# Small products at other places in TensorE's order: a later joined block in the second half, row transposes inside xa, two gate banks moved

## The chip, the cores and the metric

The kernel runs on one core of a Trainium2 chip. The core has five engines that run their own instruction streams: TensorE (PE in the profile; its weight loads are listed apart as PEld), VectorE (DVE), ScalarE (ACT), GpSimd (POOL) and SyncE (SP), which issues most of the DMAs. The metric is device time in microseconds (us) of one execution. A difference of less than about half a per cent between two versions can hardly be told from none.

## The reference

One layer of a decoder trunk on 1024 tokens of width 1024, in float32. Cut to what matters here:

```python
h = rms_norm(x, norm_mix)
xa, ga, q, f, v, g, m_a, m_b = split(h @ w_in)            # 8 projections, 1024 wide each
xa  = causal_depthwise_conv(xa, conv_w, conv_b)           # 4 taps
r   = sigmoid(blockdiag(xa, w_r) + b_r)                   # blocks of 256
i   = sigmoid(blockdiag(xa, w_i) + b_i)
a   = exp(-8 * r * softplus(-lam))
hr  = scan(h_t = a_t * h_(t-1) + sqrt(1 - a_t**2) * (i * xa)_t)
y_a = hr * gelu(ga)
# HGRN2, 8 heads of 128, chunks of 32 tokens, a state S of 128 x 128 per head
F   = lb + (1 - lb) * sigmoid(f);   K = (1 - lb) * sigmoid(-f);   Q = silu(q)
o_t = Q_t @ S_t  with  S_t = F_t * S_(t-1) + K_t (outer) v_t
y_b = rms_norm(o, hg_norm) * silu(g)
y   = sigmoid(m_a) * y_a + sigmoid(m_b) * y_b
x   = x + y @ w_out
x   = x + square(relu(rms_norm(x, norm_mlp) @ w_up)) @ w_down
out = rms_norm(x, norm_final)
```

## The kernel before

**Products.** A float32 product is made of three products of rounded parts: `mm3` issues H·H, L·H and H·L (lines 132, 133, 134). `split` makes the parts of a weight (`wH` a cast on ScalarE, L87, `wL` a subtraction on VectorE, L88). A "step" of a projection is six matmuls of 128x512.

**The mixer.** Tokens come in two halves (c = 0, 1) of T = 512, and heads in four pairs (p = 0..3) of 256 columns: eight blocks i = 4c + p. For each there is a generator `stage(i)`, which issues the work ahead of its recurrence: the products for `v` of block i−1 in four quarters tt (24 matmuls of 256 columns each, with the call `between(tt)` after a quarter), `xa` with its convolution, `q`, `f`, and `rg_lru` with the two gates (`pr`, `pi`, six matmuls each, for s = 0 and 1). `hgrn(i)` issues the recurrence of block i. It makes decay products on VectorE (`kk`, `kc`, `kb`, `qa`, `qb`, `qf`) and small products on TensorE: the level blocks `pt1`, `pt2`, `pt8`; the "joined block" of 32 rows (L634) and of 64 rows (L645) of the scores `sc`; transposes `pk` of `kk` (L671); `pkv` (L681), from which VectorE makes the states `sn` (L692); the output `po` (L706, L709). After it comes the norm of `po`: squares with a sum on ScalarE (L713), their power on GpSimd (`hrs`, L721), `normalised()` (L728). `on_T` later transposes the result (L384) and stores it in `od`. In stages 1 to 3 the rows of the second half are transposed as well (`transposed`, L162).

**The order.** While `hgrn(i)` runs, `stage(i+1)` is taken forward in pieces: `go(n)` issues its next n steps. The table

```python
GO = (26, 5, 2, 1, 1)
```

says how many steps go ahead of the level blocks, then of the joined block, of `pk`, of `pkv` and of `po`. In the mixer TensorE's instructions are pinned to the order in which they are written; the other engines' orders are made by a scheduler.

**Banks.** PSUM is shared in three groups: `pj` with four banks, `sc` with two, `hg` with two. A product waits until the bank that it takes in turn has been read. Projections take `pj`; `pt1`, `pt2` and the 64 rows take `sc`; `pt8`, the 32 rows, `pk`, `pkv`, `po` and all transposes take `hg`.

**GpSimd's other work.** From the fifth block on, `combos_on(n)` puts in n pieces that form sums of weights for the gate phase; a long piece has two products (L324), two more of `stT` and eight sums `r`.

**The gate phase.** The four gates' products (ga, m_a, m_b, g) are made in 16 "quads" of 512 x 512 by a Strassen-like scheme, of which `own` lists fourteen, 2 to 15. `gate_step(q, step)` issues step 0 to 6 of a quad: 12 matmuls into a bank X (`pj`), Y (`sc`) or Z (`hg`). Steps 0 to 2 end in a copy on ScalarE, steps 3 to 5 in an add on VectorE (L1000), step 6 in a copy. `gate_work(q)` then applies the gate's function to the whole quad (128x2048): for quad 2, the first of `own`, it is the gelu, with a TS (L1028), a product (L1029), tanh, two products (L1032) and one by the RG-LRU's `h`. `with_o(p)` multiplies the merged gate `g2` by `o` (L1057). The next quad's operands are loaded by `load_quad` (L906, in the order `in_turn`) and split (`wA`, `ws…`). The output projection and the MLP follow.

Of the kernel before, what the change touches and what calls it, by code (L numbers as in the profile page):

```python
# [14 lines left out]
ALU = mybir.AluOpType  # L15
# [17 lines left out]
OUT_TILES = 8  # L33
QUADS = 16
LEVELS = (2, 8)
GO = (26, 5, 2, 1, 1)
OWN_BEFORE = 2


# [5 lines left out]
def trunk(ctx: ExitStack, tc: tile.TileContext, x, wts, mlp, pv, gains, mask_f, mask_u, out):  # L45
    nc = tc.nc
    V, A, G, PE = nc.vector, nc.scalar, nc.gpsimd, nc.tensor
# [13 lines left out]
    def bank(tag, name):  # L61
        return ps.tile([P, 512], F32, tag=tag, name=name, bufs={"pj": 4, "sc": 2, "hg": 2}[tag])
# [3 lines left out]
    for i in range(NC * NPAIR):  # L66
        at = (0, 1, 2, 3, 4, 6, 5)
# [98 lines left out]
    hT = []  # L166
# [192 lines left out]
    def v_steps(c, p, got, between):  # L359
        v = mt("v", f"v_{c}{p}", (P, 4, 256))  # L360
        w = [next_w(), next_w()]
        for tt in range(4):
            pp = bank("pj", f"pv_{c}{p}_{tt}")
            for k in range(8):
                hh, hl = kt(hT[c], k)
                cut = slice(tt * P, (tt + 1) * P)
                cols = slice((k % 4) * 256, (k % 4 + 1) * 256)
                wh, wl = w[k // 4]
                mm3(pp[:, :256], hh[:, cut], hl[:, cut], wh[:, cols], wl[:, cols], k == 0, k == 7)
                if k % 2:  # L370
# [58 lines left out]
    def rg_lru(c, p, got, xc, xh, xl):  # L429
        wh, wl = next_w()  # L430
        nm = f"{c}{p}"
        w, ig, e = (mt(t, f"{t}{nm}", (P, 2, T)) for t in ("rw", "ri", "rr"))
        a = mt("h", f"a{nm}", (P, 2, T))
        last = []

        def on_act(*a, **k):
            ins = A.activation(*a, **k)
            if last:
                how = mybir.DependencyInfo(mybir.DependencyClass.NoSync, mybir.DependencyReason.DATA)
                tc.add_manual_dep(ins.ins, last[-1].ins.name, how, reason="on_act")  # L440
            last.append(ins)

        for s in range(2):
            u = 2 * p + s
            pr, pi = bank("pj", f"pr{c}{u}"), bank("pj", f"pi{c}{u}")
            for o, k0 in ((pr, 0), (pi, 2)):
                for k in range(2):
                    cols = slice((k0 + k) * 256 + s * P, (k0 + k) * 256 + (s + 1) * P)
                    mm3(o, wh[:, cols], wl[:, cols], xh[:, k, :], xl[:, k, :], k == 0, k == 1)
                yield  # L450
            on_act(w[:, s, :], pr, AF.Sigmoid, bias=pvt[:, PV_BR + u : PV_BR + u + 1])
            on_act(ig[:, s, :], pi, AF.Sigmoid, bias=pvt[:, PV_BI + u : PV_BI + u + 1])
# [49 lines left out]
    def hgrn(c, p, got, go):  # L502
        q1, f, kk = got["q1"], got["f"], got["kk"]
# [87 lines left out]
        t4 = nxt.rearrange("p (a b) -> p a b", b=4)  # L591
        q4 = qb.rearrange("p a (b c) -> p a b c", c=c1)
        level_q(q4, t4, g1, c1)
        go(GO[0] - (10 if first else OWN_BEFORE))
        pt1 = blocks(kk, lambda k: q1[:, 16 * k : 16 * k + 16, :], "1")
        if not first:
            go(OWN_BEFORE)
# [27 lines left out]
                op1=ALU.add,  # L625
            )

        go(GO[1])
# [38 lines left out]
        go(GO[2])  # L667
# [9 lines left out]
        go(GO[3])  # L677
# [6 lines left out]
        for s, u in both:  # L684
            sn = sns[:, s]
            states.append([scar[:, u, :]] + [sn[:, n, :] for n in range(4)])
            for n in range(nkv):
# [3 lines left out]
                else:  # L691
# [5 lines left out]
                        op0=ALU.mult,  # L697
                        op1=ALU.add,
                    )
        go(GO[4])  # L700
        po = [bank("hg", f"po{c}{u}") for _, u in both]
        for s, u in both:
            for n in range(4):
# [46 lines left out]
    def v_of(i):  # L750
        def between(tt):
            if tt == 0:
                gots[i - 1]["tail"]()
            if tt == 1:
                on_T(*where(i - 2), gots[i - 2])
            for n in {(2, 2): (1,), (3, 0): (2,), (3, 2): (3,)}.get((i, tt), ()):
                with tc.high_priority(400):
                    transposed(xn1[n], hT[1], n, f"x1{n}")

        yield from v_steps(*where(i - 1), gots[i - 1], between)  # L760

    def stage(i):
# [3 lines left out]
            yield from v_steps(c, p, got, lambda tt: None)  # L766
        elif i > 1:
            yield from v_of(i)
        px = yield from project_steps(c, f"xa{c}{p}")
        xc, xps = conv_in(c, p, px)  # L770
        if i == 0:
            parameters()
# [200 lines left out]
        loads.append(ins)  # L973

    GQ = 2 * QUADS
    gwork, gb, gbank, ge, live = {}, {}, {}, {}, {}
    SIGN = (1.0, -1.0, -1.0, 1.0)

    def gp_tile(tag, name):
# [2 lines left out]
    def gate_step(q, step):  # L982
# [12 lines left out]
        if step < 3:  # L995
            ge[q, step] = gp.tile([P, T], F32, tag="e", name=f"ge{step}_{q}", bufs=4)
            A.copy(ge[q, step], o)
        elif step < 6:
            at, e = {3: (0, 0), 4: (2, 1), 5: (3, 2)}[step]
            V.tensor_tensor(out=b[:, at, :], in0=o, in1=ge.pop((q, e)), op=ALU.add)  # L1000
        else:
            A.copy(b[:, 1, :], o)

# [9 lines left out]
    def gate_work(q):  # L1013
# [11 lines left out]
        elif gate == 2:  # L1025
            t = gp_tile("sg", f"sg{q}")
            A.activation(t, b, AF.Square)
            V.tensor_scalar(t, t, 0.044715, 1.0, op0=ALU.mult, op1=ALU.add)  # L1028
            V.tensor_tensor(out=t, in0=t, in1=b, op=ALU.mult)  # L1029
            A.activation(t, t, AF.Tanh, scale=GELU_C)  # L1030
            for cut, one in ((slice(0, 4, 3), 1.0), (slice(1, 3), -1.0)):
# [22 lines left out]

    def with_o(p):
        o = load_4(od[p], f"o{p}")
        V.tensor_tensor(out=live["g2"], in0=live["g2"], in1=o, op=ALU.mult)  # L1057

    yt = {}

# [39 lines left out]
    gwork[own[0]]["c"]()  # L1100
    live["g2"] = gp_tile("b", "g2_0")
    nc.sync.dma_start(live["g2"], g2d)
    with_o(0)
    for q in own:
        n = q + 1
        if n > own[1] and n < QUADS:
# [1 line left out]
        for step in (1, 2, 5, 4, 6) if q == own[0] else (0, 1, 2, 3, 4, 5, 6):  # L1108
# [3 lines left out]
            gate_step(q, step)  # L1112
            if q == own[0] and step == 4:
                gate_step(own[1], 0)
            pinned[0] = False
            if n == QUADS:
                if step == 2:
# [10 lines left out]
            for k in {2: ("sums", "a", "b"), 5: ("c",), 6: ("d",)}.get(step, ()):  # L1128
                if q > own[0]:
                    gwork[n][k]()  # L1130
                elif k != "a":
                    with tc.high_priority(300):
                        gwork[n][k]()
        gate_work(q)
    close_gp()
    close_tp()
    close_w1()
# [388 lines left out]
```

## Time and profile before

| | |
|---|---|
| time, median of 3 runs | 1584.06 us (1580.7 to 1586.53) |
| time of the profiled execution | 1579.99 us |
| its span, first to last instruction | 1578.2 us |
| mean granted TensorE clock | 0.997 |
| TensorE, matmul | 1528.8 us, 97% |
| VectorE | 1208.0 us, 77% |
| ScalarE | 819.6 us, 52% |
| GpSimd | 162.0 us, 10% |
| DMA | 280.07 MB, mean 177 GB/s |

The first of the gate phase's products in a bank X starts at 579.2 us; what lies before is the mixer. A row of the trace gives the start (us), the length, the engine, the source line, the operation with out<-in (numbers of names left out), its shape and, in square brackets, how long the engine stood idle before it and which instruction of which engine ended that. In a row that groups several instructions (x4) the length reaches from the first's start to the last's end, or is their sum. A busy TensorE may still be slow: the granted clock in the view of windows tells.

### The profile page before, as it was taken

How to read it: one execution, taken by the hardware profiler on the slowest of the kernel's cores; microseconds unless marked ns; L12 is line 12 of the kernel's file. 1: busy time of each engine (PE TensorE's matmuls, PEld its weight loads, DVE VectorE, ACT ScalarE, POOL GpSimd, SP SyncE). 2: the span in 40 equal slices, each digit the busy share in tenths (PEclk: the TensorE clock that was granted, in tenths of full speed). 3: DMA queues.
4: the chain of work that ended last, by engine and by line, in shares of the span. 5: the costliest groups of instructions: out<-in, count | busy, mean ns of one | idle time of the engine just before them, and what ended most of it. 6: DMA issues, size and time to landing. Idle time of an engine off the chain costs nothing.

```text
span 1578.2 us, 23146 instructions
## 1 busy us (share of the span) xinstructions
PE 1528.8 (97%) x9072; PEld 1275.6 (81%) x9072; DVE 1208.0 (77%) x1706; ACT 819.6 (52%) x1341; POOL 162.0 (10%) x187
## 2 busy tenths in 40 slices
PE   7989999999999999999999998999999999999998
PEld 6878888888787887888888876888888878888886
DVE  5797586696876928786866489987778888888877
ACT  5646656567475634444444277776777632211113
POOL 1011110234437600000000000000000000000000
PEclk9999999999999999999999999999999999999999
DMA  6333222232433364424237863766666575666642
GB/s 235 99 99 108 68 96 93 84 132 94 134 134 121 108 253 161 159 96 141 92 126 271 290 224 112 277 255 251 250 246 252 224 272 225 250 254 255 254 198 107
DMA packets 75341, 280.07 MB, mean 177 GB/s; under 512 B 7776, under 2 KB 20192, under 8 KB 62304
## 3 DMA queue, kind: packets, MB, share of 16 engines
q1 hardware_dynamic: 72208, 267.58, 46.6%
q10 hardware_dynamic: 3024, 11.01, 1.9%
q8 instruction: 71, 1.16, 0.3%
q14 instruction: 38, 0.31, 0.1%
HBM read 193.63 MB, written 84.93 MB: 177 GB/s over the span
## 4 chain that ended last, share of the span: by engine, by line
PE 75%; DVE 14%; ACT 7%; issue 2%; DMA 1%; POOL 0%; DVEq 0%; POOLq 0%; SPq 0%; ACTq 0%
PE dX L132 3%; PE dX L133 3%; PE dX L134 3%; PE uX L132 3%; PE uX L133 3%; PE uX L134 3%; PE gX L132 3%; PE gX L134 3%; PE gX L133 3%; PE dY L132 2%; PE dY L133 2%; PE dY L134 2%; PE uY L132 2%; PE uY L134 2%; PE uY L133 2%
## 5 line engine op out<-in xcount | busy, mean ns | idle before, releaser
L88 DVE TENSOR_TENSOR wL<-raw,wH 128x1024 fp32r<-128x1024 f32 x100 | 123.9, 1242 | 86.5 <-ACT wH L87 86.5
L87 ACT CAST wH<-raw 128x1024 fp32r<-128x1024 f32 x100 | 104.9, 1049 | 68.4 <-PE po L133 29.2
L1435 DVE TENSOR_TENSOR acc<-acc,dX 128x512 f32<-128x512 f32 x128 | 85.0, 682 | 29.5 <-PE dX L134 28.3
L87 ACT CAST wA<-q 128x512 fp32r<-128x512 f32 x46 | 28.4, 620 | 132.5 <-PE dX L134 101.4
L1435 DVE TENSOR_TENSOR acc<-acc,dY 128x512 f32<-128x512 f32 x64 | 43.4, 685 | 15.6 <-PE dY L134 14.5
L132 PE MATMUL po<-wH,y 128*128 128x512 f32 x128 | 50.1, 391 | 0.0
L133 PE MATMUL po<-wL,y 128*128 128x512 f32 x128 | 50.0, 391 | 0.0
L134 PE MATMUL po<-wH,y 128*128 128x512 f32 x128 | 50.0, 391 | 0.0
L1300 ACT ACTIVATE b<-b 128x512 f32<-128x512 f32 x48 | 30.1, 630 | 29.6 <-DVE b L1299 29.5
L155 POOL TENSOR_TENSOR rstd_h<-rstd_h,mhalf 128x1 f32<-128x1 f32 x8 | 5.6, 699 | 384.2 <-DVE rstd_h L154 384.2
L411 DVE SCALAR_TENSOR_TENSOR xc<-xp,pvt,xc 128x512 f32<-128x512 f32 x48 | 40.4, 862 | 0.0
L713 ACT ACTIVATE on<-po 128x128 f32<-128x128 f32 x64 | 16.8, 278 | 43.8 <-PE po L709 43.8
L88 DVE TENSOR_TENSOR wA<-q,wA 128x512 fp32r<-128x512 f32 x46 | 31.5, 685 | 9.3 <-ACT wA L87 9.2
L918 DVE TENSOR_TENSOR s<-q,q 128x512 f32<-128x512 f32 x46 | 31.5, 687 | 3.0 <-DMA q<-mlp_in 2.5
L324 POOL TENSOR_TENSOR stt<-r,stt 128x256 fp32r<-128x256 f32 x16 | 23.2, 1469 | 93.0 <-ACT stt L323 93.0
L923 DVE TENSOR_TENSOR s<-q 128x512 f32<-128x512 f32 x46 | 31.5, 685 | 0.3
L1301 ACT ACTIVATE b<-b 128x512 f32<-128x512 f32 x48 | 30.1, 630 | 1.1
L1000 DVE TENSOR_TENSOR gb<-gY,ge 128x512 f32<-128x512 f32 x14 | 9.7, 690 | 26.0 <-PE gY L134 25.4
L134 PEld LDWEIGHTS po<-wH,y 128*128 128x128 f32 x128 | 24.0, 188 | 5.0
L133 PEld LDWEIGHTS po<-wL,y 128*128 128x128 f32 x128 | 24.0, 188 | 4.9
L132 PEld LDWEIGHTS po<-wH,y 128*128 128x128 f32 x128 | 24.0, 188 | 4.8
L706 PE MATMUL po<-v,scT 128*128 128x128 f32 x128 | 24.6, 286 | 2.7 <-DVE sn L692 2.7
(2528 smaller groups left out, 5424.9 us busy)
## 6 DMA issues: line engine op xcount, KB each, us to landing
raw<-wts_in SPq DMA_DIRECT2D x96, 512.0 KB, 3.6
q<-mlp_in SPq DMA_DIRECT2D x92, 512.0 KB, 3.7
x<-x_in SPq DMA_DIRECT2D x8, 512.0 KB, 6.0
hd<-ri SPq DMA_DIRECT2D x16, 256.0 KB, 2.9
od<-onT ACTq DMA_DIRECT2D x8, 512.0 KB, 4.7
cdT<-stT SPq DMA_DIRECT2D x16, 256.0 KB, 3.5
o<-od SPq DMA_DIRECT2D x4, 1024.0 KB, 7.1
h<-hd SPq DMA_DIRECT2D x4, 1024.0 KB, 4.8
```

Source lines behind the costliest of these rows:

```text
L87: keep(A.copy(h, src))
L88: keep(V.tensor_tensor(out=lo, in0=src, in1=h.bitcast(F32), op=ALU.subtract))
L132: pin(PE.matmul(o, ah, bh, start=first, stop=False, **how))
L133: pin(PE.matmul(o, ah, bl, start=False, stop=False, **how))
L134: pin(PE.matmul(o, al, bh, start=False, stop=last, **how))
L411: ins = V.scalar_tensor_tensor(xc[:, s, :], xp[:, j : j + T], pvt[:, PV_CW + 8 * j + u : PV_CW + 8 * j + u + 1], xc[:, s, :], op0=ALU.mult ...
L706: pin(PE.matmul(on_ps, scT[:, 4 * s + n, :], vn(s, n), start=True, stop=only))
L918: V.tensor_tensor(out=sa[:, 0, :], in0=a21, in1=a22, op=ALU.add)
L923: V.tensor_tensor(out=sb[:, 0, :], in0=a21, in1=a11, op=ALU.add)
L1300: A.activation(b[:, at, :], b[:, at, :], AF.Relu, scale=-1.0 if at == 2 else 1.0)
L1301: A.activation(b[:, at, :], b[:, at, :], AF.Square)
L1435: V.tensor_tensor(out=dst, in0=dst, in1=banks[bk, pr], op=op)
```

## The change

Nothing is added to or taken from the work; every engine has as many instructions as before. What changes is where some stand.

```diff
-GO = (26, 5, 2, 1, 1)
+GO = (26, 5, 3, 1, 1)
+GO_FIRST = (16, 5, 2, 1, 2)
+GO_SECOND_HALF = (26, 7, 3, 1, 1)
...
-            pp = bank("pj", f"pv_{c}{p}_{tt}")
+            pp = bank("pj" if tt < 3 else "sc", f"pv_{c}{p}_{tt}")
...
-            pr, pi = bank("pj", f"pr{c}{u}"), bank("pj", f"pi{c}{u}")
+            pr, pi = (bank(("pj", "sc")[s], f"p{o}{c}{u}") for o in "ri")
...
-        go(GO[0] - (10 if first else OWN_BEFORE))
+        at = GO_FIRST if first else GO_SECOND_HALF if c else GO
+        go(at[0] - (0 if first else OWN_BEFORE))
...
-            if tt == 1:
+            if tt == (2 if i == 2 else 1):
                 on_T(*where(i - 2), gots[i - 2])
-            for n in {(2, 2): (1,), (3, 0): (2,), (3, 2): (3,)}.get((i, tt), ()):
+            for n in {}.get((i, tt), ()):
...
-        px = yield from project_steps(c, f"xa{c}{p}")
+        def more(n):
+            with tc.high_priority(400):
+                transposed(xn1[n], hT[1], n, f"x1{n}")
+
+        hooks = {at: lambda n=n: more(n) for at, n in {2: ((4, 1),), 3: ((2, 2), (6, 3))}.get(i, ())}
+        px = yield from hooked(project_steps(c, f"xa{c}{p}"), hooks)
...
+    def behind_steps(ins):
+        how = mybir.DependencyInfo(mybir.DependencyClass.NoSync, mybir.DependencyReason.DATA)
+        tc.add_manual_dep(ins.ins, added[own[1], 4].ins.name, how, reason="behind_steps")
...
-            V.tensor_scalar(t, t, 0.044715, 1.0, op0=ALU.mult, op1=ALU.add)
+            ins = V.tensor_scalar(t, t, 0.044715, 1.0, op0=ALU.mult, op1=ALU.add)
+            if q == own[0]:
+                behind_steps(ins)
...
-    with_o(0)
     for q in own:
...
+            if q == own[1] and step == 6:
+                with_o(0)
+                gate_work(own[0])
...
-        gate_work(q)
+        if q > own[0]:
+            gate_work(q)
```

`added[q, step]` is the add L1000 of that quad and step, and `with_o(0)` calls `behind_steps` with its product too. The other `go(GO[k])` read `at[k]`. `hooked(steps, hooks)` was there before: it calls a hook after the nth step. A dependency of the class NoSync sets the order on an engine without a semaphore. Lines of the new kernel have higher numbers, by 2 at the top, 3 in `hgrn` from `pk` on, and 14 to 16 in the gate phase.

On TensorE, at the end of block 0's recurrence (`pr` and `pi` are the gates of the next block's RG-LRU), before:

```order
L134 MATMUL pr_1147<-xcH_1080,wL_990 128x512
L706 MATMUL po_1155<-v_243,scT 128x128 x2
L709 MATMUL po_1155<-sn_1128,qf_970 128x128
L706 MATMUL po_1155<-v_243,scT 128x128
L709 MATMUL po_1155<-sn_1128,qf_970 128x128
```

and now:

```order
L136 MATMUL pr_1147<-xcH_1080,wL_990 128x512
L134 MATMUL pi_1148<-xcH_1080,wH_989 128x512
L135 MATMUL pi_1148<-xcL_1081,wH_989 128x512
L136 MATMUL pi_1148<-xcH_1080,wL_990 128x512
L134 MATMUL pi_1148<-xcH_1080,wH_989 128x512
L135 MATMUL pi_1148<-xcL_1081,wH_989 128x512
L136 MATMUL pi_1148<-xcH_1080,wL_990 128x512
L709 MATMUL po_1161<-v_243,scT 128x128 x2
L712 MATMUL po_1161<-sn_1128,qf_970 128x128
```

The six matmuls of `pi` moved from behind `po` to ahead of it.

On VectorE, in block 5's recurrence, from the last masked copy of a level block (`dd`) to the first state `sn`, before:

```order
L535 COPY_PREDICATED dd_4005<-mu,sc_11_4348 128x8x8
L506 TENSOR_TENSOR kk_3997<-kk_3997,seg_4007 128x8x64
L506 TENSOR_TENSOR qf_4392<-qf_4392,seg_4007 128x8x64
L485 SCALAR_TENSOR_TENSOR q_4496<-sq_4497,par,pj_q_0_4295 128x256x2
L88 TENSOR_TENSOR wL_4507<-raw_4504,wH_4506 128x1024
L485 SCALAR_TENSOR_TENSOR q_4496<-sq_4497,par,pj_q_1_4296 128x256x2
L692 SCALAR_TENSOR_TENSOR sn_4541<-scar,seg_4007,pkv_4533 128x128
```

and now:

```order
L537 COPY_PREDICATED dd_4005<-mu,sc_11_4348 128x8x8
L487 SCALAR_TENSOR_TENSOR q_4461<-sq_4462,par,pj_q_0_4295 128x256x2
L90 TENSOR_TENSOR wL_4472<-raw_4469,wH_4471 128x1024
L487 SCALAR_TENSOR_TENSOR q_4461<-sq_4462,par,pj_q_1_4296 128x256x2
L508 TENSOR_TENSOR kk_3997<-kk_3997,seg_4007 128x8x64
L508 TENSOR_TENSOR qf_4392<-qf_4392,seg_4007 128x8x64
L90 TENSOR_TENSOR wL_4548<-raw_4545,wH_4547 128x1024
L695 SCALAR_TENSOR_TENSOR sn_4565<-scar,seg_4007,pkv_4557 128x128
```

The next block's two `q` products and a weight's `wL` moved ahead of the halves of `kk` and `qf` (128x8x64), on which `pk` and `po` depend.

On VectorE, in the gate phase, around the adds of the second quad of `own` (quad 3), before:

```order
L923 TENSOR_TENSOR s_6332<-q_6313 128x512
L1028 TENSOR_SCALAR sg_6288<-sg_6288 128x2048
L924 TENSOR_TENSOR s_6332<-q_6314,s_6331 128x512
L1029 TENSOR_TENSOR sg_6288<-sg_6288,gb_6148 128x2048
L1057 TENSOR_TENSOR g_0_6181<-g_0_6181,o_6183 128x2048
L1032 SCALAR_TENSOR_TENSOR gb_6148<-sg_6288,gb_6148 128x2x512
L1032 SCALAR_TENSOR_TENSOR gb_6148<-sg_6288,gb_6148 128x1024
L88 TENSOR_TENSOR ws136L<-s_6331,ws136H 128x1024
L1000 TENSOR_TENSOR gb_6256<-gZ_6344,ge_3_6269 128x512
L1000 TENSOR_TENSOR gb_6256<-gX_6255,ge_3_6311 128x512
```

and now:

```order
L932 TENSOR_TENSOR s_6319<-q_6300 128x512
L933 TENSOR_TENSOR s_6319<-q_6301,s_6318 128x512
L90 TENSOR_TENSOR ws136L<-s_6318,ws136H 128x1024
L1014 TENSOR_TENSOR gb_6253<-gZ_6331,ge_3_6266 128x512
L90 TENSOR_TENSOR wA_6480<-q_6456,wA_6480 128x512
L1014 TENSOR_TENSOR gb_6253<-gX_6252,ge_3_6298 128x512
L1073 TENSOR_TENSOR g_0_6181<-g_0_6181,o_6388 128x2048
L1014 TENSOR_TENSOR gb_6253<-gY_6285,ge_3_6316 128x512
L1042 TENSOR_SCALAR sg_6391<-sg_6391 128x2048
```

The five operations of 128x2048 (or two times half of it) moved behind the add of `gX`, and the split `wA` of the next quad's load `q_6456` moved ahead of that add.

More of the change, by code (lines that the diff above doesn't have):

```diff
@@ L626, in hgrn @@
             )
-        go(GO[1])
+        go(at[1])
         pt = bank("hg", f"sc32_{nm}")[:, :256].rearrange("p (n t) -> p n t", n=8)
@@ L666, in hgrn @@
         vn = lambda s, n: got["v"][:, n, s * P : (s + 1) * P]
-        go(GO[2])
+        go(at[2])
         pk = [bank("hg", f"pk{c}{u}") for _, u in both]
@@ L676, in hgrn @@
             A.copy(kT[s][:, :nkv, :], pk[s][:, : nkv * P].rearrange("p (n k) -> p n k", n=nkv))
-        go(GO[3])
+        go(at[3])
         pkv = [bank("hg", f"pkv{c}{u}") for _, u in both]
@@ L699, in hgrn @@
                     )
-        go(GO[4])
+        go(at[4])
         po = [bank("hg", f"po{c}{u}") for _, u in both]
@@ L975, in trunk @@
     GQ = 2 * QUADS
-    gwork, gb, gbank, ge, live = {}, {}, {}, {}, {}
+    gwork, gb, gbank, ge, live, added = {}, {}, {}, {}, {}, {}
+    def behind_steps(ins):
+        how = mybir.DependencyInfo(mybir.DependencyClass.NoSync, mybir.DependencyReason.DATA)
+        tc.add_manual_dep(ins.ins, added[own[1], 4].ins.name, how, reason="behind_steps")
     SIGN = (1.0, -1.0, -1.0, 1.0)
@@ L999, in gate_step @@
             at, e = {3: (0, 0), 4: (2, 1), 5: (3, 2)}[step]
-            V.tensor_tensor(out=b[:, at, :], in0=o, in1=ge.pop((q, e)), op=ALU.add)
+            added[q, step] = V.tensor_tensor(out=b[:, at, :], in0=o, in1=ge.pop((q, e)), op=ALU.add)
         else:
@@ L1056, in with_o @@
         o = load_4(od[p], f"o{p}")
-        V.tensor_tensor(out=live["g2"], in0=live["g2"], in1=o, op=ALU.mult)
+        ins = V.tensor_tensor(out=live["g2"], in0=live["g2"], in1=o, op=ALU.mult)
+        if p == 0:
+            behind_steps(ins)
     yt = {}
```

## The prediction

> **What bounds the kernel now.** The page's line of busy times comes first.
>
> ```profile
> PE 1528.8 (97%) x9072; PEld 1275.6 (81%) x9072; DVE 1208.0 (77%) x1706; ACT 819.6 (52%) x1341; POOL 162.0 (10%) x187
> ```
>
> TensorE (PE) is busy for 1528.8 of a span of 1578.2 us. An edit that leaves its work alone can save only the 49 us in which it idles and the time lost to a lowered clock. So the next view is TensorE's waits; the columns are total us, times, longest us. These are the rows in the places that the change touches.
>
> ```profile
> PE sc L645 <- DVE qf L506: 4.7, 3, 1.6
> PE pk L671 <- DVE kk L506: 3.9, 4, 1.1
> PE po L706 <- DVE sn L692: 2.7, 1, 2.7
> PE gX L132 <- DVE gb L1000: 2.7, 1, 2.7
> PE xT_x L162 <- ACT onT L385: 1.7, 1, 1.7
> PE sc L634 <- DVE qb L506: 1.5, 3, 0.5
> PE sc L645 <- ACT scT L650: 1.4, 1, 1.4
> PE xT_x L162 <- ACT on L728: 1.4, 2, 0.9
> PE poT L384 <- ACT on L728: 1.0, 2, 0.6
> ```
>
> They add up to 21.0 us: that is what moving products can win back by waits, less 0.7 of the second row, which is block 0's and stays. Third, the windows show what the clock costs. A row gives the stretch, its length, the busy us (and instructions) of PE, PEld, DVE, ACT and POOL, the granted clock, the DMA share and GB/s.
>
> ```profile
> 111.58:114.99 3.41, 0.81 (x4) 0.34 (x2) 3.41 (x10) 1.13 (x2) 0.00 (x0) 1.00 0.70 228
> 114.99:118.41 3.42, 3.27 (x15) 3.30 (x16) 3.38 (x9) 0.00 (x0) 0.98 (x2) 0.50 0.12 43
> 620.17:623.58 3.41, 3.41 (x10) 2.64 (x9) 2.93 (x2) 0.30 (x2) 0.00 (x0) 0.50 0.22 85
> 951.26:954.67 3.41, 1.68 (x12) 1.58 (x13) 2.97 (x5) 1.81 (x5) 0.86 (x1) 1.00 0.36 147
> 954.67:958.08 3.41, 3.12 (x19) 2.44 (x17) 3.41 (x6) 2.92 (x7) 0.00 (x0) 1.00 0.26 107
> ```
>
> The stretch after block 0's wait for `po` ran at half clock, and so did the one after the gate phase's wait; each lost half of 3.4 us, 1.7. In the first row TensorE was idle for 2.60 us of 3.41 and lost the next stretch. In the fourth it was idle for 1.73 and lost nothing. The limit lies between these, so a wait that gets shorter can win 1.7 us more than its own length.
>
> **Block 0, `GO_FIRST` and the banks.** The last places go from 1 to 2, so the six matmuls of `pi` stand ahead of `po`. `pr` and `pi` of s=0 are in `pj` in both kernels; `pi` has a bank there before `po`, as the order shows. One row of block 0:
>
> ```profile
> 115.14 1.19 PE L706 MATMUL po<-v,scT 128*128 128x128 f32 x4 [2.74 <-DVE sn L692]
> ```
>
> TensorE stands for 2.74 us until VectorE has the states `sn`. Nothing that VectorE does before `sn` is moved, so `sn` keeps its time and the six matmuls fill part of the wait. For their length I use block 5, whose rows serve the next part too.
>
> ```profile
> 416.42 0.39 PE L134 MATMUL pj_q<-hT11H,wL 128*128 128x512 f32 x1
> 417.32 0.70 PE L634 MATMUL sc<-qb,kc 128*32 128x32 f32 x32 [0.52 <-DVE qb L506]
> 419.60 1.12 PE L645 MATMUL sc<-qf,kk 128*64 128x64 f32 x16 [1.57 <-DVE qf L506]
> 420.64 0.50 PE L132 MATMUL pj_q<-hT11H,wH 128*128 128x512 f32 x1
> 423.27 0.39 PE L134 MATMUL pj_f<-hT10H,wL 128*128 128x512 f32 x1
> 424.77 0.87 PE L671 MATMUL pk<-ident,kk 128*128 128x128 f32 x6 [1.11 <-DVE kk L506]
> ```
>
> The matmul at 423.27 is the twelfth from 420.64, so one takes 2.63/11 = 0.24 us and a step of six 1.4. The wait becomes 2.74 − 1.4 = 1.3, under the 1.73 that cost no clock, so the 1.7 comes back too: 3.1 us. If `sn` came later by those 1.4, the gain would be 0; if the bank move let it come earlier, 4.4. I take 3.1, since the rows ahead of `sn` are the same.
>
> At this place the Trainium skill ("TensorE: Matmul & The Clock Gate", section "HAM oscillation — how this bites in real kernels") asks only that gaps in TensorE's work stay under about 3.4 us. The two rows above at 0.50 disagree, since gaps of 2.74 us were enough. By the page the clock terms would not come from these gaps and need not return, which would take 3.4 from the sum.
>
> **Blocks 4 to 7, the joined block two steps later.** In block 5 (4 and 6 have the same three waits) TensorE idles 0.52 + 1.57 + 1.11 = 3.20 us. Now twelve matmuls more stand ahead of L634: it arrives at 416.65 + 12 × 0.24 = 419.5. `qb` is there since 417.3 and `qf` since about 419.5, so the first two waits are gone. With 0.70 + 1.04 of products it is through at 421.26, and after three steps of six at `pk`, at 425.57. But the move changes VectorE's order too. Block 5 on VectorE:
>
> ```profile
> 423.89 0.23 DVE L535 COPY_PREDICATED dd<-mu,sc 128x64 f32<-128x64 uint8 x1
> 424.03 0.68 DVE L506 TENSOR_TENSOR kk<-kk,seg 128x512 f32<-128x512 f32 x1
> 425.44 0.74 DVE L485 SCALAR_TENSOR_TENSOR q<-sq,par,pj_q 128x512 f32<-128x512 f32 x1
> 426.10 1.21 DVE L88 TENSOR_TENSOR wL<-raw,wH 128x1024 fp32r<-128x1024 f32 x1
> 427.23 0.73 DVE L485 SCALAR_TENSOR_TENSOR q<-sq,par,pj_q 128x512 f32<-128x512 f32 x1
> ```
>
> In the new order the two `q` products and `wL` stand ahead of `kk`'s halves: 425.44 to 427.89, 2.45 us (the gaps between them are none). `kk` then ends at 424.71 + 2.45 = 427.16 where `pk` wants it at 425.57: a new wait of 1.6 instead of 1.11. Per block 3.20 − 1.6 = 1.6 us, for three blocks 4.8. Block 7 waits only at L645, by `scT` of ScalarE, 1.4; twelve matmuls (2.9 us) cover that. On SP a weight load now stands ahead of four stores of combinations, which only the gate phase reads: 0. Together 6.2. The ends: 0, if everything on VectorE comes later with TensorE (the wait moves on), and 1.4 + 3 × 3.20 = 11.0, if `kk` is there in time.
>
> **Row transposes and `on_T`.** The three rows L162 and L384 of the waits, 1.7 + 1.4 + 1.0 = 4.1 us, are transposes placed in v's quarters, where ScalarE has `on` or `onT` still to write. Those of stage 2 (`on_T` one quarter later) and of rows 1 to 3 (behind a step of xa) now have 24 matmuls of 256 columns or more ahead of them. In the later stages `on_T` never waits: the last row counts two waits, both of them block 0's. I take 4.1. If the cover is gone, because ScalarE is late by as much in the new place, it is 0; the new place can also cost what it holds up in the shared `hg` banks, at worst another 4.1. The fourth v quarter's bank and the s=1 gates' go from `pj` to `sc`: these take turns with the level blocks, and no row shows a wait for such a bank, so 0, with one wait of 0.3 for each of seven stages (2 us) as the bad end.
>
> **The gate phase.** Here `g2·o`, the TS of the gelu and what follows it are put behind step 4's add of the quad `own[1]`.
>
> ```profile
> 610.08 2.28 DVE L1029 TENSOR_TENSOR sg<-sg,gb 128x2048 f32<-128x2048 f32 x1
> 614.49 2.35 DVE L1032 SCALAR_TENSOR_TENSOR gb<-sg,gb 128x1024 f32<-128x1024 f32 x2
> 618.49 0.68 DVE L1000 TENSOR_TENSOR gb<-gX,ge 128x512 f32<-128x512 f32 x1
> 637.49 0.68 DVE L1000 TENSOR_TENSOR gb<-gX,ge 128x512 f32<-128x512 f32 x1
> 619.22 0.50 PE L132 MATMUL gX<-gT4H,wA1235H 128*128 128x512 f32 x1 [2.74 <-DVE gb L1000]
> 638.90 0.39 PE L132 MATMUL gX<-gT4H,wA1236H 128*128 128x512 f32 x1
> 608.49 0.33 SPq L906 DMA_DIRECT2D q<-mlp_in  x1
> q<-mlp_in SPq DMA_DIRECT2D x92, 512.0 KB, 3.7
> ```
>
> Before, TensorE waits 2.74 us for the add of 618.49, which stands on VectorE behind L1029, L1057 and both L1032, 6.7 us (610.08 to 616.84). These go behind the add. What then is late next is the load of 608.49, whose `wA` split now stands ahead of the add: landing takes 3.7 us, so about 612.2, and with cast, split and add it ends at about 614.5 by my estimate. TensorE is at the product at about 616.5 (619.22 − 2.74) less the five matmuls of the next quad moved behind it, 615.2. The wait goes, and with it the 1.7 of the half clock: 4.4. The 6.7 us of VectorE come back a quad later: the add of 637.49 ended at 638.17, 0.7 before the matmul of 638.90 that needs its bank. TensorE comes 4.4 earlier, but has 18 matmuls (4.1) more ahead of it, and VectorE is late by some of the 6.7; from 0 to 2.6 us of new wait, 1.0 taken. The move takes a DMA along: the load of `h` (1 MB, SP) now stands behind the second half of that quad's load, and its user L1034 is moved back as far; the load of `o` keeps its place on SP, so neither is waited for, and what is moved past them, the quad's load, comes no later. Gain 3.4, with ends −1 (the load is late by all the wait, and the next quad's 2.6 comes on top less the clock) and 4.4.
>
> **Sum.** 3.1 + 6.2 + 4.1 + 3.4 = 16.8 us. The profiled execution took 1579.99 us (span 1578.2 and 1.8 around it), 4.1 less than the median of the runs, 1584.06. So 1563.2 for its like and 1567 for the median.
>
> **Rivals.** (a) *The wait only moves in blocks 4 to 7.* VectorE, 77% busy overall, is busy throughout the block's rows above, and its order sets when `kk` comes; against it, the TensorE rows have 2.1 us of waits that end before `kk`'s. Then 6.2 is lost from the sum: 1573. (b) *Slower: the power for the norm comes late.* On GpSimd (POOL) `hrs` (L721) moves behind a piece of twelve instructions (two L324 products, two `stT`, eight `r`). Block 5's rows:
>
> ```profile
> 434.85 1.65 POOL L721 TENSOR_TENSOR hrs<-hssq,mhalf 128x8 f32<-128x8 f32 x1 [7.27 <-DVE hssq L719]
> 436.47 1.68 POOL L324 TENSOR_TENSOR stt<-r,stt 128x256 fp32r<-128x256 f32 x2
> 446.83 1.60 POOL L316 TENSOR_TENSOR r<-r 128x256 f32<-128x256 f32 x1
> 447.71 2.14 ACT L728 ACTIVATE on<-po,hrs 128x128 f32<-128x128 f32 x8
> ```
>
> The piece lasts from 436.47 to about 448.4, 12 to 13.6 us between stages. L728 needs `hrs` and stands on ScalarE ahead of f's sigmoids, for which the next block's chain waits. L728 is due at 424.77 + 22.9 now, in the new order by TensorE's place some 18.6 after `pk`. If the piece starts as soon as its casts L323 are done (in the new order ahead of the squares, about 2.3 after `pk`), `hrs` ends 16 to 17.6 after `pk`: 1 to 2.6 in hand. If it starts only where it does now, 11.7 after `pk`, `hrs` ends 25.4 after, 6.8 late, three times: 20.4 us, so 16.8 − 20.4 = 3.6 slower, 1588. It turns the sign at 16.8/3 = 5.6 us of lateness per block. (c) *The clock falls otherwise.* The stretches of 3.41 us run on by themselves, and a gap of 2.4 us around 951 fell over two of them, in the last two rows of the windows, neither of which was lowered. If the timed executions mostly escape too, the two terms of 1.7 are no gain: 1571. The Trainium skill (the same page, section "What's actually happening") also has a window of about 3.4 us that doesn't start with the kernel; how it falls in a second execution no run here shows yet. (d) *More:* `kk` and the next quad's add come in time, which wins 4.8 + 1.0: 1561. (e) *Hardly anything:* the load in the gate phase and the transposes keep their waits, and (a) holds: only block 0's 3.1 us is left: 1581.
>
> **Chances.** The forecast 0.47, (a) 0.17, (c) 0.12, (d) 0.10, (e) 0.06, (b) 0.08. A change of under 0.5%, 7.9 us, can hardly be told from none in this kernel. Under 1576.1 lie the forecast, (c) and (d) nearly whole and four fifths of (a): 0.78 with what is cut off at the edges. Slower by over 7.9 is the far end of (b), and mishaps that I don't see: 0.08. The range from 1558 to 1579 leaves out (b), (e) and the best of (d), with the unlikeliest corners of (a).
>
> **What would show it.** Right: `po` of block 0 waits about 1.3 us and no stretch behind it is at 0.50; no L634 or L645 rows (in the new numbering L637, L648) among the waits; `pk` waits about 1.6 in blocks 4 to 6; no L162; no gX step in the gate phase over 1 us. Wrong: `pk` waits of 3 us (a); idle of ScalarE before L731 ended by POOL, and an f-bank wait behind it (b); half-clock stretches at other places (c); an L384 that waits on ScalarE in its new quarter.

## The result and the profile after

The changed kernel takes 1564.28 us (median of four executions, 1562.36 to 1564.69); the kernel before took 1583.93 us in its four (1580.7 to 1586.53). The ratio is 0.9879 with a 95% interval from 0.9866 to 0.9892, 1.2% faster. The forecast was 1567. The profiled executions differ by less, 1579.99 to 1564.07 us; the experiments show why.

First the page's line of busy times of the changed kernel:

```profile
PE 1523.0 (97%) x9072; PEld 1271.9 (81%) x9072; DVE 1205.4 (77%) x1706; ACT 818.5 (52%) x1341; POOL 155.5 (10%) x187
```

The instructions are the same. TensorE's own busy time is 5.8 us shorter all the same; one stretch at half clock fewer (below) can account for some 1.7 of it, the rest was not taken apart. Then TensorE's waits in the changed kernel (total us, times, longest), in the places that the change touches:

```profile
PE pk L674 <- DVE kk L508: 6.2, 4, 1.8
PE po L709 <- DVE sn L695: 1.4, 1, 1.4
PE gX L134 <- ACT ge L1011: 1.2, 1, 1.2
```

Of the nine rows shown of before, two are left, `pk` and `po`; no row of the joined block, none of a row transpose (`xT_x`) behind ScalarE, none of `poT`. One row is new, in the gate phase. The single instructions of TensorE in the changed kernel, block 0, block 5 and the gate phase (the number in brackets is the wait):

```profile
114.93 0.68 PE L709 MATMUL po<-v,scT 128*128 128x128 f32 x4 [1.38 <-DVE sn L695]
409.53 0.70 PE L637 MATMUL sc<-qb,kc 128*32 128x32 f32 x32
410.15 1.15 PE L648 MATMUL sc<-qf,kk 128*64 128x64 f32 x16
417.31 0.87 PE L674 MATMUL pk<-ident,kk 128*128 128x128 f32 x6 [1.71 <-DVE kk L508]
610.28 0.50 PE L134 MATMUL gX<-gn2H,ws136H 128*128 128x512 f32 x1 [1.23 <-ACT ge L1011]
```

Block 0's `po` waits 1.38 us instead of 2.74, the joined block not at all, `pk` 1.71 instead of 1.11. On VectorE the same place of block 5:

```profile
413.99 0.23 DVE L537 COPY_PREDICATED dd<-mu,sc 128x64 f32<-128x64 uint8 x1
414.12 0.74 DVE L487 SCALAR_TENSOR_TENSOR q<-sq,par,pj_q 128x512 f32<-128x512 f32 x1
414.78 1.22 DVE L90 TENSOR_TENSOR wL<-raw,wH 128x1024 fp32r<-128x1024 f32 x1
415.92 0.74 DVE L487 SCALAR_TENSOR_TENSOR q<-sq,par,pj_q 128x512 f32<-128x512 f32 x1
416.58 0.68 DVE L508 TENSOR_TENSOR kk<-kk,seg 128x512 f32<-128x512 f32 x1
```

`q`, `wL` and `q` run from 414.12 to 416.58, 2.46 us, and the half of `kk` ends at 417.26, just ahead of `pk`.

For the account by stage, the same two rows of a tile's instructions in both kernels, before and then after (shortest, median and longest ns, then the start of the first and of the last in us):

```profile
L132 PE MATMUL gX<-hT00H,wA x56: 389/389/476, 579.2 to 834.1; 128*128 128x512 f32 x56
L132 PE MATMUL po<-wH,y x128: 388/389/487, 851.1 to 947.0; 128*128 128x512 f32 x128
```

```profile
L134 PE MATMUL gX<-hT00H,wA x56: 389/389/476, 564.7 to 816.5; 128*128 128x512 f32 x56
L134 PE MATMUL po<-wH,y x128: 388/389/477, 833.5 to 931.4; 128*128 128x512 f32 x128
```

The gate phase starts 14.5 us earlier, the output projection 17.6 earlier, and the span ends 16.0 earlier (1578.2 to 1562.2). So the mixer won 14.5, the gate phase 3.1, and 1.6 were lost again behind, where nothing had been moved. Two more starts divide the mixer:

| first matmul of (start in us) | before | after | earlier by |
|---|---|---|---|
| `v` in stage 2, behind block 0's `po` | 124.03 | 120.90 | 3.1 |
| `pr` of block 4, behind all row transposes | 306.36 | 297.99 | 8.4 |
| the gate phase | 579.24 | 564.74 | 14.5 |

Of the first 3.1, 0.2 are there already at block 0's `pk` (105.64 and 105.43), so block 0 won 2.9 us, the stages with the row transposes 5.2 and blocks 4 to 7 6.1.

The 1.6 us behind are a balance. First the MLP's row transposes `xT_h` wait 1.9 us longer, by the rows of before and then of after:

```profile
PE xT_h L1182 <- DVE xn_h L156: 1.2, 2, 1.1
```

```profile
PE xT_h L1203 <- DVE xn_h L158: 2.0, 1, 2.0
PE xT_h L1203 <- ACT wH L89: 1.1, 1, 1.1
```

Such waits differ between executions of one program: in the second profiles of the two kernels, of which more below, they come to 2.5 and 2.1 us. The other loss is in the windows of the changed kernel (columns as in the prediction):

```profile
114.99:118.41 3.42, 3.42 (x30) 3.38 (x31) 3.39 (x9) 1.65 (x10) 0.84 (x2) 1.00 0.02 6
934.93:938.34 3.41, 1.02 (x10) 0.99 (x10) 2.97 (x6) 1.84 (x5) 0.86 (x1) 1.00 0.54 221
938.34:941.75 3.41, 3.41 (x10) 2.64 (x10) 3.41 (x5) 2.43 (x5) 0.00 (x0) 0.50 0.14 24
```

Behind block 0's wait the clock stays full. But the old 2.4 us gap, which in the profile of before lay over two windows around 951 us, now fell into one, and the next 3.41 us ran at half clock. That cost 1.6 us: the lead is 15.6 at the MLP's first `uX` (947.73 and 932.11) and 14.1 at its first `uZ` (958.00 and 943.94). Of these 3.5 us 1.9 come back by the end, most of them where TensorE waited 1.0 us for `h2t1` in the first profile and does not in this one.

### The profile page after: what moved, and what is told of

It reads as the page before. It is cut to its first block, busy times and chain, and to the rows that moved or that the text cites. A ratio compares the mean times of both kernels' runs of the same rounds, so it can differ in the third digit from the quotient of the medians.

```text
span 1562.2 us, 23154 instructions
## 1 busy us (share of the span) xinstructions
PE 1523.0 (97%) x9072; PEld 1271.9 (81%) x9072; DVE 1205.4 (77%) x1706; ACT 818.5 (52%) x1341; POOL 155.5 (10%) x187
## 4 chain that ended last, share of the span: by engine, by line
PE 79%; DVE 11%; ACT 6%; issue 2%; DMA 2%; POOL 0%; DVEq 0%; SPq 0%; ACTq 0%; POOLq 0%
PE dX L134 4%; PE dX L135 4%; PE dX L136 4%; PE uX L134 3%; PE uX L135 3%; PE uX L136 3%; PE gX L134 3%; PE gX L135 3%; PE gX L136 3%; PE dY L135 2%; PE dY L136 2%; PE dY L134 2%; PE uY L134 2%; PE uY L135 2%; PE uY L136 2%
## 5 line engine op out<-in xcount | busy, mean ns | idle before, releaser
L1456 DVE TENSOR_TENSOR acc<-acc,dY 128x512 f32<-128x512 f32 x64 | 43.5, 686 | 15.7 <-PE dY L136 14.5
L90 DVE TENSOR_TENSOR wA<-q,wA 128x512 fp32r<-128x512 f32 x46 | 31.6, 687 | 13.6 <-ACT wA L89 13.6
L615 ACT COPY kk<-kc 128x512 f32<-128x512 f32 x8 | 5.0, 622 | 43.1 <-DVE kc L508 43.1
L622 POOL TENSOR_SCALAR scT<-dd 32x256 f32<-32x256 f32 x32 | 21.5, 671 | 52.7 <-DVE dd L537 36.1
```

Source lines behind the costliest of these rows:

```text
L90: keep(V.tensor_tensor(out=lo, in0=src, in1=h.bitcast(F32), op=ALU.subtract))
L622: G.tensor_scalar(scT[32 * b : 32 * b + 32, :, 32 * b : 32 * b + 32], dd[32 * b : 32 * b + 32, :, :], 1.0, 0.0, op0=ALU.mult, op1=ALU.add,)
L1456: V.tensor_tensor(out=dst, in0=dst, in1=banks[bk, pr], op=op)
```

## Experiments

**The four parts alone**, each put into the kernel before. They ran on one chip; the kernel before took 1581.46 us there, a median of 29 executions, 2.5 less than the four executions above.

Block 0's table:

```diff
+GO_FIRST = (16, 5, 2, 1, 2)
...
+        at = GO_FIRST if first else GO
```

> The kernel before with block 0's table (16, 5, 2, 1, 2) alone. My theory, that each part wins the wait it covers: pi stands ahead of po, po waits 1.4 us instead of 2.74, no stretch at 0.50 follows, 3.1 us less, about 1581. The rival that the wait only goes to another place (pi waits for a bank in pj, or VectorE's sn comes later by as much): a wait of 1 us or more at pi or 2.7 at po, and no gain.

1580.86 us, ratio 0.9992 [0.9979, 1.0005]: hardly anything. TensorE's waits in this run:

```profile
PE poT L385 <- ACT on L730: 1.8, 2, 1.5
PE xT_x L163 <- ACT onT L386: 2.0, 2, 1.7
PE po L708 <- DVE sn L694: 1.4, 1, 1.4
```

`po` waits 1.4 as expected, and nothing waits at `pi`. But `poT` now waits 1.8 us instead of 1.0, and `xT_x` behind `onT` 2.0 instead of 1.7. ScalarE writes `on` when it did before; TensorE comes earlier and waits there. Of the 1.37 us, 1.1 are given back in stage 2. What is left is 0.3 us and the stretch at half clock, which the first profile of before has and this one has not; over twelve executions the times don't tell the two from zero. My theory that each part wins its own wait was wrong for this part.

The row transposes and `on_T`:

```diff
-            if tt == 1:
+            if tt == (2 if i == 2 else 1):
...
-            for n in {(2, 2): (1,), (3, 0): (2,), (3, 2): (3,)}.get((i, tt), ()):
...
+        hooks = {at: lambda n=n: more(n) for at, n in {2: ((4, 1),), 3: ((2, 2), (6, 3))}.get(i, ())}
+        px = yield from hooked(project_steps(c, f"xa{c}{p}"), hooks)
```

> The kernel before with the row transposes and on_T at their new places alone. My theory: the L162 and L384 waits on ScalarE go, at most one new wait of 0.3 for a bank of f in stage 3, 4.1 to 4.6 us less, about 1579.5. The rival that they wait at the new places too, or hold up xa through the hg banks: waits of 1 us and more in xa's steps of stages 2 and 3, and less than 2 us of gain.

1575.72 us, ratio 0.9962 [0.9949, 0.9974], by it 6.0 us less (4.1 to 8.1). No wait on ScalarE is left at L162 or L384, and none came in the steps of xa. From the first `v` of stage 2 to `pr` of block 4 TensorE takes 177.1 us (122.24 to 299.32) where before it took 182.3: 5.2 us, 1.1 more than the waits that went. Where these 1.1 lie the rows of waits don't show.

The second half's table, without the banks:

```diff
+GO_SECOND_HALF = (26, 7, 3, 1, 1)
...
+        at = GO_FIRST if first else GO_SECOND_HALF if c else GO
```

with `GO_FIRST` as the kernel before had it, (16, 5, 2, 1, 1).

> The kernel before with the table (26, 7, 3, 1, 1) for c = 1 alone, no bank moved. My theory: the L634 and L645 waits go, pk waits 1.7 to 1.8 us in blocks 4 to 6, about 6.8 us less, 1577. The rival that the bank moves are what lets the later joined block win: new waits of 0.5 us and more per block for banks of pj, and a gain under 4 us. The rival that the norm's power on GpSimd comes late shows as ScalarE waiting on GpSimd ahead of the normalisation.

1574.25 us, ratio 0.9954 [0.9936, 0.9972], by it 7.3 us less (4.4 to 10.1). Its waits:

```profile
PE pk L674 <- DVE kk L508: 6.1, 4, 1.7
PE pr L134 <- ACT rw L439: 1.3, 3, 0.4
```

The joined block's waits are gone and `pk` waits as in the whole change. `pr` of the second gate waits 0.4 us in three blocks, for a bank of `pj` that ScalarE still reads. From `pr` of block 4 to the gate phase's first product TensorE takes 268.9 us here (306.40 to 575.30), 272.9 before and 266.8 in the changed kernel. So without the banks the later joined block wins 4.0 us in its place, not the 6.1 of the whole change; the rest of the 7.3, as far as its interval lets one speak of it, is likely the clock's, which is argued and not shown. ScalarE never waits for GpSimd ahead of the normalisation.

The gate phase's part:

```diff
+            if q == own[0]:
+                behind_steps(ins)
...
-    with_o(0)
...
+            if q == own[1] and step == 6:
+                with_o(0)
+                gate_work(own[0])
```

> The kernel before with the gate phase's part alone. My theory: the gX wait of 2.74 us and the stretch at 0.50 behind it go, a new wait of about 1.2 us comes in the next quad behind a copy of ge on ScalarE, 3.2 us less, about 1581. The rival that only the clock matters: the gain is 1.7 or 0 by where the windows fall, and no wait of over 2 us in this place in either kernel decides it. The four parts alone add up to 17 to 18 us.

1578.85 us, ratio 0.9978 [0.9966, 0.9990], by it 3.5 us less. The `gX` wait on VectorE is gone and one of 1.1 us on ScalarE has come. By the ratios the four parts alone are 1.3 + 6.0 + 7.3 + 3.5 = 18.1 us of 1581.46; the whole change has 0.0121, 19.1. Each of these gains is known to within 2 to 3 us only, so the sum tells no more than that nothing large is missing. The profile of this run has three more stretches at 0.50, in blocks 4 to 6, whose instructions are the same as before on every engine. That called for the kernel before once more.

**The kernel before again**, without an edit.

> The kernel before once more, for a second profile of the same program. If the stretches of lowered clock and the speed of VectorE beside GpSimd are set by the program, they lie where they lay: after 114.99 and 620.17 us. If the window of the clock runs by itself, they lie elsewhere in part, between none and all of the waits of about 2 us and more (block 0, blocks 4 to 6, the gate phase, 951 us), each worth 1.7 us.

It took 1583.24 us, span 1581.4. One block, in this profile and then in the first one of the same program:

```profile
416.72:420.13 3.41, 1.36 (x38) 0.88 (x37) 3.41 (x5) 1.56 (x2) 3.17 (x4) 1.00 0.00 0
420.13:423.55 3.42, 3.42 (x20) 2.94 (x19) 3.42 (x4) 2.51 (x5) 1.33 (x2) 0.50 0.00 0
```

```profile
415.37:418.78 3.41, 2.13 (x39) 1.47 (x37) 3.41 (x4) 1.94 (x3) 3.25 (x4) 1.00 0.00 0
418.78:422.19 3.41, 2.59 (x23) 2.30 (x24) 3.41 (x5) 1.61 (x4) 2.24 (x3) 1.00 0.00 0
```

The waits at the joined block are the same, 0.5 and 1.57 us. Here they fall into one window, 2.05 us idle, and the next runs at half clock; there they fall over two, 1.28 and less, and nothing follows. This profile has such stretches behind block 0, blocks 4 to 7 and the gate wait, the first one had two (the last few us of the kernel, where TensorE runs out of work, left aside). A block loses less than the 1.7, since `pk` then no longer waits: the four stretches in blocks 4 to 7 delay the gate phase by 2.7 us together (581.92 against 579.24). So the time of the kernel before depends on where the windows fall, and it spreads from 1578.7 to 1589.5 over the runs of this study. Of the 29 executions on one chip the three with a mean clock of 0.989 or 0.990 took 1584.6 to 1587.8, the nine with 0.996 or 0.997 took 1578.8 to 1581.4. Within the first profile the two lowered stretches lie 148 times 3.413 us apart; those of the second lie at another phase. The Trainium skill ("TensorE: Matmul & The Clock Gate", section "What's actually happening") says that the window of about 3.4 us runs freely; the two profiles agree.

**The banks put back** in the changed kernel.

```diff
-            pp = bank("pj" if tt < 3 else "sc", f"pv_{c}{p}_{tt}")
+            pp = bank("pj", f"pv_{c}{p}_{tt}")
...
-            pr, pi = (bank(("pj", "sc")[s], f"p{o}{c}{u}") for o in "ri")
+            pr, pi = (bank("pj", f"p{o}{c}{u}") for o in "ri")
```

> The changed kernel with all of v's quarters and all gates back in pj. The run of the second half's table alone showed pr of s=1 waiting 0.42 us (0.58 with the step) for a bank of pj in blocks 4 to 6. If that is the worth of the bank moves: the same waits here, 1.75 us more, about 1566 us. If the move of the banks is worth nothing as I forecast: no wait at pr and 1564.3. If it is what makes the whole change win: several waits of over 1 us on pj and 1568 or more.

```profile
PE pk L674 <- DVE kk L508: 5.8, 4, 1.7
PE pr L134 <- ACT rw L439: 1.3, 3, 0.4
```

The three waits at `pr` are back. The time, 1564.83 us, is not to be told from 1564.28; the span is 1563.6 against 1562.2. The moved banks are worth some 1.3 us by the waits and 2.1 by TensorE's places: from `pr` of block 4 to the gate phase it takes 268.8 us here (298.11 to 566.95), as in the run of the second half's table alone, and 266.8 in the changed kernel. The new 3 in `GO`, for blocks 1 to 3, was not tried by itself; no `pk` waits there in either kernel, and the stretch from `v` in stage 2 to `pr` of block 4 takes 177.1 us with it as with the rows alone.

**kk ahead of q**, in the changed kernel: an order without a semaphore puts the next block's two `q` products behind the half of `kk` for c = 1.

```diff
+        ahead = mul(halves(kk)[:, :, 0, :], halves(kk)[:, :, 0, :], t16[:, :, 1:2].to_broadcast([P, 8, 64]))
+        if c and p + 1 < NPAIR:
+            for ins in gots[NPAIR * c + p + 1]["q_ins"]:
+                tc.add_manual_dep(ins.ins, ahead.ins.name, how, reason="kk_first")
```

> The changed kernel with the next block's two q products behind the half of kk on VectorE in blocks 4 to 6. My theory, that pk waits for kk because q, wL and q stand ahead of it: two of these three go behind it, kk comes 1.2 us earlier, pk waits 0.5 us instead of 1.7, 3.7 us less, about 1560.5. The rival that kk waits for something else (the bank read of the 64 rows, GpSimd slowing VectorE): pk still waits over 1.2 us and the time stays near 1564.

1562.68 us, ratio 0.9872 [0.9852, 0.9891], by the times not to be told from the changed kernel. `pk` still waits 1.1 to 1.2 us in the three blocks, 0.6 less and not 1.2. The `wL` ahead of `kk` had stood behind the first `q`; alone it waits 0.4 us for its cast on ScalarE, and `kk` itself took 0.88 instead of 0.68. So `kk` does come earlier when less stands ahead of it, but the price was not the sum of the two moved operations. This run's profile also has 1.9 us of waits in block 7 that the changed kernel's has not; what they are stands at the end.

**kk ahead of q, pk a step later, and a copy ahead of a tanh.** The second half's table becomes (26, 7, 4, 1, 1), and in the gate phase the tanh of quad 2 is put behind the copy of `ge` of quad 4's step 0. The rows of ScalarE there, in the changed kernel:

```profile
607.84 1.91 ACT L1046 ACTIVATE sg<-sg 128x2048 f32<-128x2048 f32 x1 [1.74 <-DVE sg L1045]
609.65 0.57 ACT L1011 COPY ge<-gX 128x512 f32<-128x512 f32 x1
```

```diff
-GO_SECOND_HALF = (26, 7, 3, 1, 1)
+GO_SECOND_HALF = (26, 7, 4, 1, 1)
...
+            if q == own[2] and step == 0:
+                tc.add_manual_dep(tanhs[own[0]].ins, copied[q, 0].ins.name, how, reason="copy_first")
```

> The changed kernel with kk ahead of q, pk one step later in the second half (26, 7, 4, 1, 1), and in the gate phase the tanh of the first own quad behind the copy of ge that TensorE waits for. If each wait is what it seems: no pk wait in blocks 4 to 6 (1.9 with the step, three times) and no gX wait on ScalarE (1.4): 5.6 + 1.4 = 7 us less, 1557. The rival that the waits move on to po, to the transposes or to the next quad: less than half of it, 1561 or more.

1558.61 us, ratio 0.9850 [0.9832, 0.9868]: 5.7 us under the changed kernel's first median. The changed kernel was not run beside it; the run with the banks put back was, on the same chip, and its four executions took 1564.22 to 1565.41 against 1557.46 to 1560.10 here. Its waits:

```profile
PE gX L135 <- DMA gT4L<-cdT: 1.2, 1, 1.2
PE pv L134 <- ACT kk L500: 0.9, 3, 0.3
PE pk L679 <- DVE kk L509: 0.9, 1, 0.9
```

`pk` waits in block 0 alone, and the copy of `ge` no longer. In their place come 0.3 us three times for a bank that ScalarE reads, and the gate phase, which starts earlier still, waits 1.2 us for a load. Block 7 has 1.1 us of new waits, of the kind told at the end.

**Block 0's table put back, and the rows put back**, in the changed kernel, beside the changed kernel itself.

```diff
-GO_FIRST = (16, 5, 2, 1, 2)
+GO_FIRST = (16, 5, 2, 1, 1)
```

> The changed kernel with block 0's table put back to (16, 5, 2, 1, 1). Block 0's table alone won hardly anything, and its trace shows why: the 1.37 us won at po came back at the transposes of on_T (1.47 us of wait instead of 0.65) and of xT (0.27). If that is so, the same table is worth its whole 1.37 where on_T stands one quarter later: here po waits 2.74 again, the transposes of stage 2 don't wait, and the time is 1.4 us longer, or 3.1 where the stretch behind po falls to 0.50. The rival that the table is worth nothing in either kernel: the same time as the changed kernel's.

The second undoes the row transposes' hunks.

> The changed kernel with the row transposes and on_T put back into v's quarters. If the parts only add: 4.7 us more, as the row part alone has in its waits. If they lean on each other as I think, block 0's 1.37 is lost too, since poT waits 1.4 us instead of 0.65 for the normalised rows: about 6 us more than the changed kernel.

> The changed kernel once more beside the two runs in which a part is put back, and for a second profile. Its waits should be the same; of stretches at 0.50 it can have those behind the waits of about 2 us near 887 and 934 us and no other, so that its times spread over 3 to 4 us where those of the kernel before spread over 9.

The changed kernel took 1563.68 us here (1563.42 to 1564.19), with the block 0 table back 1566.72 and with the rows back 1571.06. The ratios to the kernel before are 0.9880 [0.9856, 0.9903], 0.9900 [0.9879, 0.9920] and 0.9922 [0.9904, 0.9940]. With the rows back, the waits are those of block 0's table alone:

```profile
PE xT_x L164 <- ACT onT L387: 2.0, 2, 1.7
PE poT L386 <- ACT on L731: 1.8, 2, 1.4
PE po L709 <- DVE sn L695: 1.4, 1, 1.4
PE xT_x L164 <- ACT on L731: 1.4, 2, 0.9
```

With the table back `po` waits 2.7, the stretch behind it runs at half clock, and no transpose waits on ScalarE. So the table is worth 3.0 us where the rows stand at their new places, and next to nothing where they don't; the rows, 6.0 us alone, are worth 7.4 here, 5.2 of it by the first, second and fourth of these rows. The intervals of the ratios overlap, though no execution of the changed kernel here (up to 1564.19) is as long as one of the other two (from 1565.58); and the profile with the table back has the same 1.9 us of waits in block 7 as the one above, so the waits carry this more than the times. The changed kernel's second profile has the same waits as its first and, within what can move, one stretch at 0.50, near 937 us. Its four times spread over 0.8 us, less than was expected.

## Why the prediction was right

**Block 0.** A `po` wait of 1.3 was forecast and 1.38 came, with a full clock behind it; in TensorE's places 2.9 us of the 3.1 came. The step took 1.73 us of idle time as safe, which it is not: in other profiles of this study windows with 1.58 and 1.69 us idle were followed by a stretch at half clock. The 1.38 lies below these, so the conclusion held. What the step did not see is that this gain stands only because another part of the same change moved the transposes: alone it comes back one stage later. The sum put the parts side by side, and was right here because all of them were in.

**Blocks 4 to 7.** `qb` and `qf` in time, the three waits at L634 and L645 gone, block 7's too, and a new `pk` wait of 1.6: measured 1.71 to 1.79. The step's reading of VectorE's order, 2.45 us of `q`, `wL`, `q` ahead of `kk`, measured 2.46. The gain was put at 6.2 and came at 6.1, but in part by luck, as the next paragraph tells.

**Rows and on_T.** 4.1 us of waits, all gone; the places show 5.2. One thing was mis-sized beside them: the bank moves, costed at 0 with the reason that no row of before shows a wait for such a bank. That was true only at the old place. With the joined block two steps later, `pr` does wait, 0.43 us in three blocks, and the bank move is what takes this away. Without the moved banks the joined block wins 4.0 us in its place, in both runs that leave them out; with them it wins 6.1. So of the forecast 6.2 about 2 us belong to the banks, which stood at 0: two errors of opposite sign, both in the sum.

**Gate phase.** The wait and the stretch at half clock went, and about 1 us was forecast as new; 1.23 came, so the sign of no `gX` step over 1 us was not met. The stage won 3.1 of the forecast 3.4. The new wait's place was the next quad, as said, but its cause was another: not VectorE's late add, but a copy on ScalarE that stood behind the tanh of 1.91 us. The tanh itself had waited 1.74 us for VectorE's product L1045, so VectorE's lateness reached TensorE by way of ScalarE. The load, which could have been late, was not, though with nothing to spare: the add that had waited ended at 600.53 in the changed kernel, by the row

```profile
599.85 0.68 DVE L1014 TENSOR_TENSOR gb<-gX,ge 128x512 f32<-128x512 f32 x1
```

and with the 14.5 us by which everything there is earlier that is 615.0 on the scale of before, where I had put it at 614.5 and TensorE at 615.2. TensorE's product starts at 600.59.

**The sum.** 16.8 us was forecast for the profiled execution and 16.0 came: 14.5 + 3.1 where the change was made, and 1.6 lost behind, for which the sum had nothing. Its terms were 3.1, 6.2, 4.1 and 3.4; 2.9, 6.1, 5.2 and 3.1 came. The medians differ by 19.7 because the kernel before seldom has as few lowered stretches as in the profile on which the sum was made: 4 of the 29 executions reach its mean clock of 0.997. Between the second profiles of the two kernels, 1581.4 and 1561.7, the difference is 19.7 too, and there nothing is lost behind the gate phase.

**The rivals.** (a) did not come: the three waits became one, and that one only 0.6 longer. (b) did not come either, and with more in hand than I gave it. The rows of GpSimd and ScalarE in block 5 of the changed kernel:

```profile
419.20 1.42 POOL L326 TENSOR_TENSOR stt<-r,stt 128x256 fp32r<-128x256 f32 x2 [1.67 <-issue]
427.36 0.74 POOL L318 TENSOR_TENSOR r<-r 128x256 f32<-128x256 f32 x1
428.06 1.66 POOL L724 TENSOR_TENSOR hrs<-hssq,mhalf 128x8 f32<-128x8 f32 x1
436.18 1.11 ACT L731 ACTIVATE on<-po,hrs 128x128 f32<-128x128 f32 x4
```

The piece starts 1.9 us after `pk` and takes 8.9 us, not 12 to 13.6; `hrs` is there at 429.72, 6.5 us before it is wanted. I had taken the piece's length from a place where a sum `r` took up to 1.60 us; here each takes about 0.73. (c) was right in its mechanism and wrong in its sign: the windows do fall otherwise from run to run, and on the average that costs the kernel before more than the first profile shows. Its example was read a window off: the gap around 951 reaches from 950.6 to 953.0, over the row of 951.26 and the window ahead of it, not over the last two rows. (d) was not in the change, but in the order: the experiment with `pk` later, `kk` earlier and the copy ahead of the tanh won 5.1 to 5.7 us (by the changed kernel's two medians) of the 5.8 that it was priced at, though the waits that went and came are partly others.

## What to carry to other kernels

A gain at one wait lasts only as far as the next product that waits on an engine whose time has not changed; list the waits behind it, and move or cover those in the same edit. Put a long operation behind the short ones that TensorE waits for on each engine in turn, since the queue that is late next may be another engine's. Where the clock is lowered by idle time, one profile shows one draw: count the waits that could lower it, and compare medians of several executions. Ask whether a bank is free at the product's new place; that none was waited for at the old one says nothing about it.

## What was not expected of the hardware

**The clock's window.** In the thirteen profiles of this study, from 100 us on, windows of 3.41 us with 1.97 us or more of TensorE's idle time were all followed by a stretch at half clock, and below 1.58 us none was; between them both occur. The Trainium skill ("TensorE: Matmul & The Clock Gate", section "HAM oscillation — how this bites in real kernels") asks for no gap above about 3.4 us; here two waits of 0.5 and 1.57 us in one window were enough.

**VectorE and GpSimd slow each other, and which one gives way changes from run to run.** In block 7 the kernel before and the run with the gate part alone have the same instructions in the same order on both engines. GpSimd in the one and in the other:

```profile
526.71 8.06 POOL L324 TENSOR_TENSOR stt<-r,stt 128x256 fp32r<-128x256 f32 x1 [13.54 <-ACT stt L323]
```

```profile
526.91 3.84 POOL L324 TENSOR_TENSOR stt<-r,stt 128x256 fp32r<-128x256 f32 x2 [13.54 <-ACT stt L323]
```

and VectorE beside it:

```profile
530.25 0.42 DVE L506 TENSOR_TENSOR qb<-qa,seg 128x256 f32<-128x256 f32 x1
```

```profile
530.07 0.96 DVE L506 TENSOR_TENSOR qb<-qa,seg 128x256 f32<-128x256 f32 x1
```

In the one, a GpSimd product that takes 0.71 us elsewhere (1.42 for two, above) stood for 8.06 while VectorE ran at full speed; in the other GpSimd got in, and VectorE's product took 0.96 instead of 0.42. TensorE then waited up to 2.7 us for `qb` in block 7 where it had not before. The Trainium skill ("SBUF — State Buffer", section "🔬 SBUF: two separate sides") says that the two share a pair of ports as an exclusive lock, which goes to whichever starts first, for the whole of its instruction. The rows agree that one stands while the other runs. But by that rule alone the GpSimd product would have come in behind the VectorE instruction that it met, and in the first profile it stood while a dozen of them ran. In four of the thirteen profiles the pair of GpSimd products took 3.7 to 3.9 us, in the other nine 7.9 to 9.7; what decides it is not shown, and that makes such a place uncertain in any forecast.
